# Early up-products for every pair, operands split ahead of two stage borders, and a modulation vector summed by columns, in a two-layer hybrid decoder

## The chip, the cores and the metric

The kernel runs on one core of one Trainium2 chip. The metric is the device time in microseconds of one execution, taken as the median of several. The engines are called as the profile calls them: PE is TensorE (PEld its weight loads), DVE is VectorE, ACT is ScalarE, POOL is GpSimd, and SP is the queue that issues nearly all DMAs.

## What is computed

Two layers of a decoder over 1024 tokens of width 1024, all in float32. Each layer has a token-mixing part and a channel-mixing part, each between two norms, with a scale, a shift and a gate that come from a vector `c`:

```python
mod = silu(c) @ ada_w[l] + ada_b[l]          # six vectors of 1024: shift, scale, gate, twice
h = rms_norm(x, g_pre_mix) * (1 + scale_m) + shift_m
q, k, v, u = split(h @ w_in + b_in)          # 512, 128, 128, 512 columns
mix = concat([window_attention(rotary(q), rotary(k), v), pool_mixer(u)]) @ w_out
x = x + gate_m * rms_norm(mix, g_post_mix)
h = rms_norm(x, g_pre_ffn) * (1 + scale_f) + shift_f
f = (silu(h @ w_gate) * (h @ w_up)) @ w_down # inner width 2816
x = x + gate_f * rms_norm(f, g_post_ffn)
```

## The kernel before

**Number format.** Every operand of a large product is split into two float32r parts: `split` (L211) lets ACT round it to `hi` (L213), and DVE subtracts to get `lo` (L214). `mm3` (L238) then issues three matmuls, hi·hi (L239), hi·lo (L242) and lo·hi (L243). A product can thus start when ACT has made `hi`, and goes on when DVE has made `lo`.

**Channel mixing.** The tokens are two halves of 512. The two large products of channel mixing are each done in a seven-product scheme (Strassen-Winograd), with the token half and the halves of the inner dimension as the two-by-two blocks. There are `NPAIR` = 11 pairs of 128-column blocks of the inner dimension. For each pair the up stage needs seven products; `double` (L989) is one of them, 24 matmuls. Two of the seven, with the right operands `B11` and `B21`, use only the first token half. For the first `sum(FIRST)` pairs they are made early by `up_firsts` (L1009): it loads the pair's first 128 columns of `w_gate` and `w_up`, adds the two products (L1034, L1036), sends the sum to DRAM (`firsts_x`, L1038), applies the gate function (L1006, L1007) and sends that as `a11` (L1042). `up_pair` (L1045) later loads these two back (L1057, L1058). A pair that was not done early makes both products itself (L1073 to L1082), so that it has seven products and not five.

**Order of the stages in one layer.** (1) q, k and v of half 0; (2) u of half 0 and attention and pooling of half 0, beside the projections of half 1; (3) the output projection of half 0 and its norm; (4) `u_pass` of half 1 beside `first_half` (L1368), which transposes the normed half 0 into eight pieces `hT`; (5) `firsts[0]`, early products for three pairs, beside attention and pooling of half 1; (6) the output projection of half 1; (7) `firsts[1]`, early products for six more pairs, beside `second_norm` (L1398), which norms half 1 and builds the 40 right operands `T2`, `T1`, `T3`, `B22`, `T4` of the up stage in `up_sums` (L971, on DVE, ACT and POOL); (8) the up stage, `up_pair` for 11 pairs; (9) the down stage, `down` (L1134), seven products over 11 pairs, in which the other half's last norm and the next layer's first pieces are made (`between`, L1458). At the end of layer 0 `post_ffn` (L538) finishes half 1.

**What sets the order.** `run` (L596) steps one main stream and lets side streams step at given rates; this is the written order. A scheduler then orders each engine's instructions, so that what is ready early can move ahead of what was written before it; each engine works its own list strictly in that order. Memory is taken from pools by tag with a fixed number of buffers; `region` (L109) frees one stage's pool and opens the next one's in the same bytes, and a tile there waits until the tiles it covers are done. `raw`, `hi`, `lo`, `ph`, `ar`, `sa`, `sb`, `fn`, `hT` and `ada` are shared by all stages; `bh` and `bl` belong to the region `down`, `cfa` and `cfb` to `mix`, the right operands `t1` to `t4` to `up`.

**The places that the change touches.** `up_firsts` splits its first operand (L1023) before its first product; the stream's first step is taken after `first_half` is done. `down` splits the first left operand (`left_of`, L1182) and right operand (L1220, into `bh` and `ph`) after the region `up` is closed. `ada_pair` (L359) makes the scale and the shift: `ada_sum` (L260) multiplies 128 × 512 blocks of `ada_w` with `c` on DVE, adding eight of them into `acc` (L271, L273), splits `acc` into two `ph` tiles, and two matmuls with a one-column selector (`picks`, L367, L368) sum over partitions; after four such rows one copy and four transposes (L375) bring the result into columns. For layer 1's first norm this runs beside the down stage of layer 0, at three steps for each of the 20 its four rows have, over 77 steps of the main stream: `(side, 3 * len(jobs) * ADA)` is 60. `normalise` (L456) scales a half by its inverse norm; at the end of layer 0 the half 1 goes from there to DRAM (L465) and comes back transposable, 128 columns at a time (L481), in the next layer's `u_pass`.

Of the kernel before, what the change touches and what calls it, by code (L numbers as in the profile page):

```python
# [20 lines left out]
P = 128  # L21
# [44 lines left out]
def hybrid_decoder_kernel(  # L66
# [193 lines left out]
    def ada_sum(l, n0, got):  # L260
# [22 lines left out]
        got += [t_("ph", [P, 512], F32R), t_("ph", [P, 512], F32R)]  # L283
        split(*got, acc)
# [104 lines left out]

    gates = {}  # L390
# [31 lines left out]
    def ada_stream(jobs):  # L422

        for l, n0, close in jobs:
            got = []
            yield from ada_sum(l, n0, got)
            close(*got)


    spill, normed = {}, {}  # L430
# [25 lines left out]
    def normalise(h, xs, rstd, keep=False):  # L456

        dst = None if keep else dr.tile([T, D], F32, tag=f"n{h}", name=f"n{h}", bufs=2)
        for t in range(NT):
            if t % 2 == 0:  # L460
                last = nc.vector.tensor_scalar(xs[t], xs[t], rstd[:, t : t + 1], None, op0=ALU.mult)
            else:
                nc.scalar.activation(xs[t], xs[t], AF.Copy, scale=rstd[:, t : t + 1])
            if not keep:
                nc.sync.dma_start(dst[t * P : (t + 1) * P, :], xs[t])  # L465
        normed[h] = dst
        return last

    def pre_norm_raw(h, k, ab, prev=None, xs=None, hf=None, bank=None):

        if bank is None:
            bank = transposed(h, k, prev, xs)
        hf = part("raw") if hf is None else hf
        scale, shift = ab[:, 0, k : k + 1], ab[:, 1, k : k + 1]
        nc.scalar.activation(hf, bank, AF.Identity, bias=shift, scale=scale)
        return hf

    def transposed(h, k, prev=None, xs=None):
        if xs is None:
            xk = part("raw").rearrange("p (t n) -> p t n", t=NT)  # L480
            nc.sync.dma_start(  # L481
                xk, normed[h].rearrange("(t p) n -> p t n", p=P)[:, :, k * P : (k + 1) * P]
            )
            src = [xk[:, t, :] for t in range(NT)]
        else:
            src = [xt[:, k * P : (k + 1) * P] for xt in xs]
# [7 lines left out]
    def pre_norm_piece(h, k, ab, prev=None, xs=None, keep=None, hf=None, bank=None):  # L494

        hf = pre_norm_raw(h, k, ab, prev, xs, hf, bank)
# [6 lines left out]

    def load_residual(h, tag="cfa"):

        xs = []
        for t in range(NT):
            if t % 2 == 0:
                big = t_(tag, [P, 4, T]).rearrange("p (t i) n -> p t (i n)", t=2)
            nc.sync.dma_start(big[:, t % 2, :], spill[h][t * P : (t + 1) * P, :])  # L510
            xs.append(big[:, t % 2, :])
        return xs

    def post_norm(h, fn, ss, xs):
# [15 lines left out]
        normalise(h, fn, inv_rms(sq), True)  # L530
# [7 lines left out]
    def post_ffn(h, fn, ss, G, keep):  # L538
# [15 lines left out]
        normalise(h, fn, inv_rms(sq), keep)  # L554
# [579 lines left out]
    def down(l, wd, load, kept, fn, ended, last):  # L1134
# [47 lines left out]
        def left_of(a, p0, p1, c0, c1):  # L1182

            n, w = p1 - p0, c1 - c0
            raw, lh, ll = (
                part(tag, 2 * w).rearrange("p (i n) -> p i n", n=w)[:, :n, :] for tag in ("raw", "hi", "lo")
            )
            nc.sync.dma_start(raw, kept[a][:, p0:p1, c0:c1])
            split(lh, ll, raw)
            return lh, ll  # L1190

# [18 lines left out]
        for name, a, right, evict in jobs[:-1]:  # L1210
            banks = [acc_bank() for _ in range(NT)]
            for g, (p0, p1) in enumerate(DOWN_GROUPS):
                n = p1 - p0
                lh, ll = left_of(a, p0, p1, 0, T)
                src = right(g)
                rights = []
                for i in range(n):
# [15 lines left out]
        for ts in ((0, 1), (2, 3)) if last else (range(NT),):  # L1233
            banks = {t: acc_bank() for t in ts}
            for g, (p0, p1) in enumerate(DOWN_GROUPS):
                n = p1 - p0
                lh, ll = left_of(a, p0, p1, ts[0] * P, (ts[-1] + 1) * P)
# [37 lines left out]
    normalise(0, xs, stats(xs, t_("rs", [P, 8])), True)  # L1275
# [5 lines left out]
    def first_pieces(b):  # L1281
        ks = (2 * b, 2 * b + 1)
        bank = transposed(0, ks[0], None, xs)
        ada_first_ab(b * CW, acc, par["cols"], par["abm"])
        for k, bank in zip(ks, (bank, None)):
            hf = t_("uT", [P, HALO + T])[:, :T]
            hts[0].append(pre_norm_piece(0, k, par["abm"], None, xs, None, hf, bank))
# [25 lines left out]
    normalise(1, xs1, rstd1, True)  # L1313
# [5 lines left out]
    FIRST = (3, 6)  # L1319
    for l in range(DEPTH):  # L1320
        cols = par["cols"]
        if l:
            region("mix")
# [3 lines left out]
        def piece_read(k, ins):  # L1327
            pieces[k] = pre_norm_piece(1, k, par["abm"], ins, None if l else xs1)
# [46 lines left out]
        pre = first_half()  # L1375
# [3 lines left out]
        ops = {B11: hts0[:HK], B21: hts0[HK:]}  # L1379
# [18 lines left out]
        def second_norm():  # L1398
# [3 lines left out]
            for k in range(HK):  # L1402
                f0, f1 = (
                    pre_norm_raw(1, kk, par["abf"], None, fn, part_)
# [29 lines left out]

        region("down")
# [22 lines left out]
        def between():  # L1458
# [10 lines left out]
            yield from post_ffn(0, fn[0], ss[0], G, True)  # L1469
# [47 lines left out]
```

## Time and profile before

| | |
|---|---|
| median of 3 runs | 1948.76 us (1945.44 to 1952.4) |
| the profiled execution, its own time | 1944.55 us |
| its span, first to last instruction | 1942.8 us |
| mean granted TensorE clock | 0.993 |
| busy: PE, DVE, ACT, POOL | 1874.0, 1564.3, 954.5, 49.0 us |
| DMA | 336.62 MB, mean 173 GB/s |

In the views, a row of a timeline gives the start and the length in us, the engine, the line, the operation, what it writes and reads, and in brackets how long its engine stood idle before it and who ended that. A row of the windows gives, for a stretch, each engine's busy time with the number of its instructions (the x in brackets), the clock that TensorE was granted (PEclk, 1.00 is full), and the share and rate of the DMA engines. Matmul records overlap, because they are pipelined: the time from the start of one to the start of the next is the pitch, and it is shorter than a record.

The stages of layer 0 end at about 75 (q, k, v), 275 (stage 4), 433 (stage 7), 762 (up) and 990 us (down); those of layer 1 at about 1232 (stage 4), 1388 (stage 7), 1720 (up) and 1943 us.

### The profile page before, as it was taken

Reading aid. Unit: us, or ns where it says so; the run is one execution under the profiler, and the core shown is the slowest. Engines: PE = TensorE matmul, PEld = TensorE weight load, DVE = VectorE, ACT = ScalarE, POOL = GpSimd, SP = SyncE. Lnnn points to the kernel's source line nnn. Section 1 sums busy time; section 2 is a strip of 40 time slices with the busy share of each in tenths; the row PEclk is TensorE's granted clock in tenths of the full one; section 3 lists DMA queues with packets and bytes.
Section 4 is the critical chain, followed back from the end, with each engine's and each line's share of the span. In section 5 each row is a group of like instructions: output and inputs, shape, how many; then the busy total and the mean of one; then the engine's idle time right before and its main releaser. Section 6 shows DMA issues by size and latency. Waiting matters only on the chain. (4 is left out here: it accounts for less than half of the span.)

```text
span 1942.8 us, 26040 instructions
## 1 busy us (share of the span) xinstructions
PE 1874.0 (96%) x8958; PEld 1541.0 (79%) x8958; DVE 1564.3 (81%) x2907; ACT 954.5 (49%) x1794; POOL 49.0 (3%) x100
## 2 busy tenths in 40 slices
PE   6999999999999999999999999999999999999997
PEld 4887778878888887778887878888778888878886
DVE  5999986779889886887878998756988888667687
ACT  4776785652222223445657668755522222235452
POOL 1000000020000000000000000000200000000000
PEclk9999999999999999999999999999999999999999
DMA  9345463556455446842556455535554644474343
GB/s 324 98 156 161 163 204 125 182 184 203 163 173 176 167 163 240 301 131 83 189 171 203 132 176 180 172 120 195 187 177 158 220 165 152 163 263 149 114 140 110
DMA packets 222052, 336.62 MB, mean 173 GB/s; under 512 B 16696, under 2 KB 120008, under 8 KB 221920
## 3 DMA queue, kind: packets, MB, share of 16 engines
q1 hardware_dynamic: 221776, 334.92, 52.2%
q8 instruction: 70, 1.15, 0.2%
q14 instruction: 62, 0.51, 0.1%
q0 software_dynamic: 32, 0.00, 0.0%
q10 hardware_dynamic: 112, 0.04, 0.0%
HBM read 262.00 MB, written 72.89 MB: 172 GB/s over the span
## 5 line engine op out<-in xcount | busy, mean ns | idle before, releaser
L213 ACT ACTIVATE hi<-raw 128x1024 fp32r<-128x1024 f32 (+1 forms) x388 | 332.5, 869 | 377.8 <-PE acc L242 220.7
L214 DVE TENSOR_TENSOR lo<-raw,hi 128x1024 fp32r<-128x1024 f32 (+1 forms) x388 | 382.9, 993 | 113.4 <-ACT hi L213 112.6
L239 PE MATMUL acc<-t,hi 128*128 128x512 f32 x704 | 276.7, 393 | 5.7 <-ACT hi L213 5.7
L243 PE MATMUL acc<-t,lo 128*128 128x512 f32 x704 | 276.1, 393 | 3.4 <-DVE lo L214 3.4
L242 PE MATMUL acc<-t,hi 128*128 128x512 f32 x704 | 276.0, 392 | 0.0
L243 PE MATMUL acc<-bh,lo 128*128 128x512 f32 x528 | 206.4, 391 | 0.0
L239 PE MATMUL acc<-bh,hi 128*128 128x512 f32 x528 | 203.5, 390 | 3.0 <-ACT bh L213 3.0
L239 PE MATMUL acc<-hT,hi 128*128 128x512 f32 x480 | 191.2, 398 | 7.8 <-ACT hi L213 7.2
L1068 DVE TENSOR_TENSOR fn<-acc,fn 128x512 f32<-128x512 f32 x220 | 151.1, 687 | 50.8 <-PE acc L243 50.2
L242 PE MATMUL acc<-hT,hi 128*128 128x512 f32 x480 | 188.3, 392 | 0.0
L243 PE MATMUL acc<-hT,lo 128*128 128x512 f32 x480 | 186.8, 393 | 0.9 <-DVE lo L214 0.9
L239 PEld LDWEIGHTS acc<-t,hi 128*128 128x128 f32 x704 | 133.5, 190 | 34.9 <-ACT hi L213 7.3
L243 PEld LDWEIGHTS acc<-t,lo 128*128 128x128 f32 x704 | 133.4, 190 | 34.2 <-DVE lo L214 6.5
L242 PEld LDWEIGHTS acc<-t,hi 128*128 128x128 f32 x704 | 133.5, 190 | 27.9
L242 PE MATMUL acc<-ph,hi 128*128 128x512 f32 x320 | 126.0, 394 | 1.3 <-DVE ph L214 1.1
L239 PEld LDWEIGHTS acc<-bh,hi 128*128 128x128 f32 x528 | 99.1, 188 | 24.6 <-ACT bh L213 3.8
L273 DVE SCALAR_TENSOR_TENSOR ada<-ar,c_act,ada 128x512 f32<-128x512 f32 x140 | 104.7, 748 | 17.0 <-DMA ar<-in_ada_w_dram 15.8
L243 PEld LDWEIGHTS acc<-bh,lo 128*128 128x128 f32 x528 | 99.6, 189 | 20.5
L239 PEld LDWEIGHTS acc<-hT,hi 128*128 128x128 f32 x480 | 90.7, 189 | 27.4 <-ACT hi L213 9.1
L1006 ACT ACTIVATE fn<-fn 128x512 f32<-128x512 f32 x44 | 27.9, 633 | 168.9 <-DVE fn L1068 168.9
L243 PEld LDWEIGHTS acc<-hT,lo 128*128 128x128 f32 x480 | 90.1, 188 | 19.5 <-DVE lo L214 1.3
L242 PEld LDWEIGHTS acc<-hT,hi 128*128 128x128 f32 x480 | 90.7, 189 | 17.3 <-issue 0.2
(302 smaller groups left out, 3866.6 us busy)
## 6 DMA issues: line engine op xcount, KB each, us to landing
ar<-in_ada_w_dram SPq DMA_DIRECT2D x160, 256.0 KB
raw<-in_w_gate_dram SPq DMA_DIRECT2D x44, 512.0 KB
raw<-in_w_up_dram SPq DMA_DIRECT2D x44, 512.0 KB
raw<-in_w_in_dram SPq DMA_DIRECT2D x80, 256.0 KB
raw<-keeps SPq DMA_DIRECT2D x40, 512.0 KB
keeps<-fn SPq DMA_DIRECT2D x66, 256.0 KB
two_b<-in_w_down_dram SPq DMA_DIRECT2D x30, 512.0 KB
raw<-keepa SPq DMA_DIRECT2D x25, 512.0 KB
```

What stands on the lines that cost most here:

```text
L213: nc.scalar.activation(hi, src, AF.Copy)
L214: nc.vector.tensor_sub(lo, src, hi.bitcast(F32))
L239: ins = nc.tensor.matmul(dst, lh, rh, start=first, stop=False)
L242: nc.tensor.matmul(dst, lh, rl, start=False, stop=False)
L243: return nc.tensor.matmul(dst, ll, rh, start=False, stop=last)
L273: nc.vector.scalar_tensor_tensor(acc, w, c_act[:, i : i + 1], acc, op0=ALU.mult, op1=ALU.add)
L1006: nc.scalar.activation(g, g, AF.Silu)
L1068: nc.vector.tensor_add(halves_of(dst)[m], bank, halves_of(src)[m])
```

## The change

Five edits, whose line numbers are those of the changed file where they are not in the kernel above.

1. `FIRST` goes from (3, 6) to (3, 8): early products for all 11 pairs. `second_norm`'s 12 steps are spread over 16 products instead of 12.
2. The first operand of `firsts[0]` is loaded and split inside `first_half`, after the sixth of the eight pieces, and not after all of them.
3. `down_prelude` loads and splits the down stage's first left and right operand before the region `up` is closed; the right one goes to two `ph` tiles instead of `bh` and `ph`. With edit 1 the right operands `hT` are also free when the early products end.
4. For layer 1's first norm `ada_columns` takes the place of `ada_pair`: `acc` isn't split; its four 128 × 128 blocks are the stationary operands of matmuls with a column of ones, whose sums land as columns. Its side stream has 28 steps over the 77 instead of 60.
5. At the end of layer 0 the region `mix` is opened before half 1's last norm, and `normalise` writes into two `cfb` tiles there; the next layer's transposes read them (as layer 0 reads its input), with no way through DRAM.

```diff
-    FIRST = (3, 6)
+    FIRST = (3, NPAIR - 3)
...
             for k in range(KD):
-                hts0.append(pre_norm_piece(0, k, par["abf"], None, fn, kept0[k]))
+                hts0.append(pre_norm_piece(k, par["abf"], None, fn, kept0[k]))
+                if k == KD - 3:
+                    next(firsts[0])
                 yield
...
-        run(firsts[0], 1 + 2 * FIRST[0], (att, ATT_STEPS), (pool, POOL_STEPS))
+        run(firsts[0], 2 * FIRST[0], (att, ATT_STEPS), (pool, POOL_STEPS))
...
+    def down_prelude(wd, kept):
+        left = left_of(kept["a11"], *DOWN_GROUPS[0], 0, T)
+        right = t_("ph", [P, 512], F32R), t_("ph", [P, 512], F32R)
+        split(*right, wd[B11][0][:, 0, :])
+        return left, right
...
+        prelude = down_prelude(wd, kept)
         region("down")
...
+    def ada_columns(l, sub, cols, ab):
+        def close(r, acc):
+            bank = msc_bank()
+            for i in range(4):
+                nc.tensor.matmul(
+                    bank[:, i : i + 1], acc[:, i * P : (i + 1) * P], ones[:, 0:1], start=True, stop=True
+                )
+            m, o = r // 2, slice(r % 2 * 4, r % 2 * 4 + 4)
+            k0 = (3 * sub + 1 - m) * KD
+            nc.vector.tensor_add(ab[:, m, o], bank[:, 0:4], cols[:, k0 + o.start : k0 + o.stop])
+            if m == 0:
+                ada_scale(ab, sub, o, cols)
...
-            jobs = ada_pair(l + 1, 0, nxt["cols"], nxt["abm"])
+            jobs = ada_columns(l + 1, 0, nxt["cols"], nxt["abm"])
...
-            (between(), 7 * NPAIR), (side, 3 * len(jobs) * ADA),
+            (between(), 7 * NPAIR), (side, 28),
         )
         if nxt:
-            drain(post_ffn(1, fn[1], ss[1], G, False))
+            region("mix")
+            xs1 = wide_tiles("cfb")
+            drain(post_ffn(1, fn[1], ss[1], G, xs1))
```

What it moves shows in the engines' lists. The first place is DVE in layer 0 where `firsts[1]` ends and the up stage begins. `t_...`, `b` and the sums into `ar` and `sa` at L979 and L984 are `up_sums`; L1036 adds the last early product; L1083, L1084 and the `lo<-raw` behind them prepare the first product of the up stage. Before:

```order
L214 TENSOR_TENSOR t_4507<-sa,t_4506 128x512
L214 TENSOR_TENSOR t_4539<-ar,t_4538 128x512
L1007 TENSOR_TENSOR sb<-sb 128x512
L1083 TENSOR_TENSOR raw<-raw 128x8x128
L979 TENSOR_TENSOR ar<-sa,ar 128x512
L214 TENSOR_TENSOR b_4533<-sa,b_4532 128x512
L1084 TENSOR_TENSOR raw<-raw 128x8x128
L214 TENSOR_TENSOR t_4517<-ar,t_4516 128x512
L214 TENSOR_TENSOR t_4525<-sa,t_4524 128x512
L984 TENSOR_TENSOR sa<-sa,ar 128x512
L214 TENSOR_TENSOR lo<-raw,hi 128x1024
L214 TENSOR_TENSOR t_4509<-sa,t_4508 128x512
```

In the changed kernel the same place of DVE's list (L1054 is the addition of the early product, L1101, L1102 and L1106 are the preparations):

```order
L214 TENSOR_TENSOR t_4584<-sa,t_4583 128x512
L214 TENSOR_TENSOR t_4616<-ar,t_4615 128x512
L1054 TENSOR_TENSOR sb<-acc,sa 128x512
L1025 TENSOR_TENSOR sb<-sb 128x512
L1101 TENSOR_TENSOR raw<-raw 128x8x128
L271 TENSOR_SCALAR ada<-ar,c_act 128x512
L1102 TENSOR_TENSOR raw<-raw 128x8x128
L273 SCALAR_TENSOR_TENSOR ada<-ar,c_act,ada 128x512
L1106 TENSOR_TENSOR raw<-raw 128x8x128
L214 TENSOR_TENSOR lo<-raw,hi 128x1024
L273 SCALAR_TENSOR_TENSOR ada<-ar,c_act,ada 128x512
L1054 TENSOR_TENSOR sb<-acc,sa 128x512
```

All of `up_sums` now stands ahead of the preparations, and the first product's `lo` ahead of the last early product's additions; operations of the next modulation vector (`ada`) have moved in between.

The second place is ACT in layer 0 behind `u_pass` of half 1 (`uT` are its results). `raw<-msc` and `hT<-raw` are pieces of `first_half`, and `hi<-raw 128x1024` is the operand of the first early product. Before:

```order
L684 ACTIVATE uT<-acc,cols 128x512 x4
L475 ACTIVATE raw<-msc,colp 128x512 x2
L213 ACTIVATE hT<-raw 128x512 x2
L475 ACTIVATE raw<-msc,colp 128x512
L213 ACTIVATE hi<-raw 128x1024
L213 ACTIVATE hT<-raw 128x512
```

In the changed kernel:

```order
L702 ACTIVATE uT<-acc,cols 128x512 x4
L495 ACTIVATE raw<-msc,colp 128x512 x2
L213 ACTIVATE hT<-raw 128x512
L213 ACTIVATE hi<-raw 128x1024
L213 ACTIVATE hT<-raw 128x512
L495 ACTIVATE raw<-msc,colp 128x512
```

The operand has moved ahead by one `hT` split and one `raw` copy. PE's list is the same in both kernels up to the first early product.

The third place is SP's list at the start of layer 0's up stage in the changed kernel; L1071 loads the weights of a pair, `ar<-in_ada_w_dram` those of the modulation, and `hT<-in_w_down_dram` the right operand `B11` of the down stage:

```order
L1076 DMA sa<-keepa_2926 128x512
L280 DMA ar<-in_ada_w_dram 128x512
L1147 DMA hT<-in_w_down_dram 128x512
L1147 DMA hT<-in_w_down_dram 128x2x512
L1056 DMA firsts<-sa 128x1024
L280 DMA ar<-in_ada_w_dram 128x512 x2
L1147 DMA hT<-in_w_down_dram 128x2x512
L1076 DMA sa<-keepa_2926 128x512
L1060 DMA keepa_2926<-sb 128x512
L1147 DMA hT<-in_w_down_dram 128x2x512
L1071 DMA raw<-in_w_gate_dram 128x4x256
L1071 DMA raw<-in_w_up_dram 128x4x256
```

The loads of `B11` stood at the end of the up stage before; now four of the six stand ahead of the second pair's weights.

More of the change, by code (lines that the diff above doesn't have):

```diff
@@ L282, in ada_sum @@
                 yield
-        got += [t_("ph", [P, 512], F32R), t_("ph", [P, 512], F32R)]
-        split(*got, acc)
+        if whole:
+            got.append(acc)
+        else:
+            got += [t_("ph", [P, 512], F32R), t_("ph", [P, 512], F32R)]
+            split(*got, acc)
         yield
@@ L388, in ada_pair @@
         ]
+    def ada_columns(l, sub, cols, ab):
[10 more added lines that the diff above has]
+                ada_scale(ab, sub, o, cols)
+        return [
+            (l, (3 * sub + 1 - r // 2) * D + r % 2 * 512, lambda acc, r=r: close(r, acc), True)
+            for r in range(4)
+        ]
     gates = {}
@@ L422, in ada_stream @@
     def ada_stream(jobs):
[L424 removed]
+        for l, n0, close, *whole in jobs:
             got = []
[L426 removed]
+            yield from ada_sum(l, n0, got, *whole)
             close(*got)
[L430 removed]
+    spill = {}
     for h in range(NHALF):
@@ L476, in pre_norm_raw, with transposed @@
         return hf
[L478 to L486, printed above, removed]
+    def transposed(k, prev, xs):
+        src = [xt[:, k * P : (k + 1) * P] for xt in xs]
         bank = msc_bank()
@@ L536, in scaled_add, with post_ffn @@
         nc.vector.tensor_add(fn, fn, xt)
-    def post_ffn(h, fn, ss, G, keep):
+    def post_ffn(h, fn, ss, G, into=None):
         rstd = inv_rms(ss)
@@ L553, in post_ffn @@
         spill[h] = new
-        normalise(h, fn, inv_rms(sq), keep)
+        normalise(fn, inv_rms(sq), into)
         yield
@@ L1132, in down_loads, with left_of, down @@
         return wd, load
-    def down(l, wd, load, kept, fn, ended, last):
+    def left_of(a, p0, p1, c0, c1):
+        n, w = p1 - p0, c1 - c0
+        raw, lh, ll = (
+            part(tag, 2 * w).rearrange("p (i n) -> p i n", n=w)[:, :n, :] for tag in ("raw", "hi", "lo")
+        )
+        nc.sync.dma_start(raw, a[:, p0:p1, c0:c1])
+        split(lh, ll, raw)
+        return lh, ll
+    def down_prelude(wd, kept):
[3 more added lines that the diff above has]
+        return left, right
+    def down(l, wd, load, kept, fn, ended, last, prelude):
         (c11, c12), (c21, c22) = [[[c[:, i * 512 : (i + 1) * 512] for c in fn[h]] for i in range(2)] for h in range(2)]
@@ L1213, in down @@
                 n = p1 - p0
[L1214 to L1217, printed above, removed]
+                if name == "p1" and g == 0:
+                    (lh, ll), *rights = prelude
+                else:
+                    lh, ll = left_of(kept[a], p0, p1, 0, T)
+                    src = right(g)
+                    rights = []
+                for i in range(len(rights), n):
                     rights.append((t_("bh", [P, 512], F32R), t_("ph" if count[0] % 5 < 3 else "bl", [P, 512], F32R)))
@@ L1327, in piece_read @@
         def piece_read(k, ins):
-            pieces[k] = pre_norm_piece(1, k, par["abm"], ins, None if l else xs1)
+            pieces[k] = pre_norm_piece(k, par["abm"], ins, xs1)
         qkvs = {h: [] for h in range(NHALF)}
```

74 lines of the change are left out of this document (33 added, 41 removed).

## The prediction

> **What bounds the kernel now.** I read the page's busy times first, then a calm stretch of the windows as a yardstick, then PE's waits, and last the windows and timeline around each border.
>
> ```profile
> span 1942.8 us, 26040 instructions
> PE 1874.0 (96%) x8958; PEld 1541.0 (79%) x8958; DVE 1564.3 (81%) x2907; ACT 954.5 (49%) x1794; POOL 49.0 (3%) x100
> ```
>
> PE is the bound on average, and only 69 us of the span are without a matmul. None of the five edits removes a large product, so what can be won is where PE stands still or runs below its usual pace. The yardstick is layer 1's up stage:
>
> ```profile
> 1432.00:1720.00 288.00, 288.00 (x1271) 237.65 (x1269) 233.50 (x299) 77.71 (x90) 0.00 (x0) 1.00 0.50 169
> ```
>
> Here PE is full at a full clock: 288.00 / 1271 = 0.2266 us for each matmul. For any other stretch of 128 × 512 matmuls, the lost time is its width less 0.2266 times its matmuls; this counts idle time and slow clock together. Now the waits of PE (columns: total us, times, longest):
>
> ```profile
> PE acc L239 <- ACT hi L213: 14.6, 9, 3.1
> PE msc L367 <- ACT ph L213: 3.7, 6, 1.4
> PE acc L239 <- ACT bh L213: 3.0, 2, 1.5
> PE msc L368 <- DVE ph L214: 2.3, 3, 1.3
> PE msc L489 <- DMA raw<-n: 1.3, 1, 1.3
> ```
>
> Each of these has an edit: `hi` late (edits 1 and 2), `bh` late (3), `ph` of the modulation late (4), half 1's way through DRAM (5). They add up to 24.9 us, and the stretches around them lose more than the waits themselves. They are on the path, because PE's list is in order and nothing else is due there.
>
> **Edit 1, early products to up stage.**
>
> ```profile
> 430.00:447.00 17.00, 13.75 (x46) 10.00 (x45) 16.82 (x22) 7.79 (x11) 3.75 (x2) 0.80 0.47 157
> 1386.00:1403.00 17.00, 13.00 (x43) 9.36 (x42) 16.85 (x20) 8.24 (x12) 3.73 (x2) 0.80 0.42 140
> ```
> ```profile
> 434.71 0.50 PE L239 MATMUL acc<-t,hi 128*128 128x512 f32 x1 [1.75 <-ACT hi L213]
> 436.57 0.79 PE L243 MATMUL acc<-t,lo 128*128 128x512 f32 x1 [1.12 <-DVE lo L214]
> ```
> ```profile
> 431.25 2.32 DVE L1084 TENSOR_TENSOR raw<-raw 128x1024 f32<-128x1024 f32 x1
> 435.30 1.21 DVE L214 TENSOR_TENSOR lo<-raw,hi 128x1024 fp32r<-128x1024 f32 x1
> 438.34 0.69 DVE L214 TENSOR_TENSOR t<-ar,t 128x512 fp32r<-128x512 f32 x1
> ```
>
> DVE is full (16.82 of 17.00) while PE waits: the releaser `hi` of ACT is itself fed by DVE's L1084, which ended at 433.57. DVE is still in `up_sums` until 438.34 + 0.69 = 439.03, while PE's first idle began at 434.71 - 1.75 = 432.96. DVE is 6.1 us behind. The stretch loses 17.00 - 46 × 0.2266 = 6.6 us in layer 0 and 17.00 - 43 × 0.2266 = 7.3 us in layer 1.
>
> Two pairs more are four products of 24 matmuls, 96 × 0.2266 = 21.8 us more under which DVE can finish. DVE gets work with them: I allow per product one `lo` (1.21) and two additions (0.69), 10.4 us for four, and four modulation steps that moved in, at 0.748:
>
> ```profile
> L273 DVE SCALAR_TENSOR_TENSOR ada<-ar,c_act,ada 128x512 f32<-128x512 f32 x140 | 104.7, 748 | 17.0 <-DMA ar<-in_ada_w_dram 15.8
> ```
>
> 21.8 - 10.4 - 3.0 = 8.4 us, more than the 6.1 it is behind, with 2.3 to spare. What is late next is the operand after the border, whose weights come by DMA. In layer 1 pair 1 already loses:
>
> ```profile
> 1426.00:1432.00 6.00, 4.15 (x18) 2.81 (x17) 6.00 (x9) 2.95 (x3) 0.00 (x0) 1.00 0.61 219
> 1416.65 1.23 DVE L1083 TENSOR_TENSOR raw<-raw 128x1024 f32<-128x1024 f32 x1 [2.66 <-DMA keepa<-sb]
> ```
>
> That is 6.00 - 18 × 0.2266 = 1.9 us, a leftover of the same backlog: DVE stood 2.66 us for a load, then was full. In sum 6.6 + 7.3 + 1.9 = 15.8 us; I keep 1.0 per layer for the first product's own wait, so **13.8** (6 if DVE catches up only by half, 15.8 at most).
>
> **Edit 3, up to down.**
>
> ```profile
> 760.00:766.00 6.00, 4.51 (x20) 3.42 (x19) 5.49 (x9) 4.30 (x7) 0.00 (x0) 1.00 0.95 299
> 763.62 1.20 PE L239 MATMUL acc<-bh,hi 128*128 128x512 f32 x4 [1.49 <-ACT bh L213]
> 1718.00:1724.00 6.00, 4.51 (x20) 3.38 (x20) 5.49 (x10) 4.30 (x7) 0.00 (x0) 1.00 0.91 295
> ```
>
> Each stretch loses 6.00 - 20 × 0.2266 = 1.5 us, all of it the wait for `bh`, whose memory lay under the last up operand. Split into `ph` it is ready before. I keep 0.2 each for the buffer it now shares: **2.6** (0 to 3.0).
>
> **Edit 4, the modulation by columns.**
>
> ```profile
> 796.00:847.00 51.00, 45.85 (x190) 35.66 (x189) 43.76 (x60) 21.89 (x37) 0.00 (x0) 0.97 0.74 246
> 839.21 0.39 PE L367 MATMUL msc<-ph,picks 128*4 128x512 f32 x1 [1.35 <-ACT ph L213]
> 840.89 0.39 PE L368 MATMUL msc<-ph,picks 128*4 128x512 f32 x1 [1.29 <-DVE ph L214]
> 43.61 0.61 PE L344 MATMUL msc<-ones_r,ar 128*128 128x1 f32 x5
> ```
>
> The four rows of the modulation put ACT's and DVE's splits into PE's path; the stretch loses 51.00 - 190 × 0.2266 = 7.9 us, about 1.7 of it the pace of the small matmuls themselves (eight at 0.2266). The new sums need no split. Their price has a near row: one-column f32 matmuls with a 128 × 128 weight, five in 0.61 us, 0.12 each. Sixteen products in two records each are 32 × 0.12 = 3.8 us; eight removed `picks` matmuls (1.8) and the transposes (some 0.5) go off, net 1.5. I keep 1.0 for waits on `acc`. 7.9 - 1.5 - 1.0 = **5.4** (2 to 7).
>
> **Edit 2, `u_pass` to early products.**
>
> ```profile
> 272.00:279.00 7.00, 5.00 (x19) 3.93 (x19) 4.98 (x12) 7.00 (x18) 0.00 (x0) 0.76 0.67 221
> 275.37 0.80 PE L239 MATMUL acc<-hT,hi 128*128 128x512 f32 x1 [2.00 <-ACT hi L213]
> 1229.00:1236.00 7.00, 5.00 (x29) 3.93 (x28) 5.94 (x18) 7.00 (x19) 0.33 (x1) 1.00 0.69 228
> 1231.90 0.50 PE L239 MATMUL acc<-hT,hi 128*128 128x512 f32 x1 [2.00 <-ACT hi L213]
> ```
> ```profile
> 273.56 0.81 ACT L475 ACTIVATE raw<-msc,colp 128x512 f32<-128x512 f32 x1
> 274.22 1.09 ACT L213 ACTIVATE hi<-raw 128x1024 fp32r<-128x1024 f32 x1
> ```
>
> ACT is full (7.00 of 7.00), so its order decides. The operand moves ahead of one copy (273.56 to 274.22, a pitch of 0.66) and one `hT` split (some 0.54, as a 512-column split is half of the 1.09): 1.2 us earlier in each layer, 2.4. In layer 0 the idle is also followed by slow clock: 0.76 over 7.00 us is 0.24 × 7.00 = 1.7 us. With 0.8 us of idle left I take two thirds of that, 1.1. Together **3.5** (1 to 5.7, the whole idle and clock). The two `hT` pieces that it passes are needed only for the last of the product's eight groups of matmuls.
>
> Short idles cost clock only sometimes: after the same 2.00 us the clock was 0.76 in one layer and 1.00 in the other, and 0.80 at both borders above. [...]
>
> **Edit 5, layer 0 to layer 1.**
>
> ```profile
> 1024.00:1043.00 19.00, 15.59 (x88) 12.00 (x88) 16.09 (x60) 14.25 (x32) 0.00 (x0) 1.00 0.60 182
> ```
>
> PE is idle for 19.00 - 15.59 = 3.4 us around the read-back of half 1; 1.3 of that is the wait for `raw<-n` above, which goes. Of the other 2.1, short waits for `hi`, `lo` and a norm, I take half: **2.3** (0 to 3.4).
>
> **What it adds.**
>
> ```profile
> raw<-in_w_gate_dram SPq DMA_DIRECT2D x36, 256.0 KB
> firsts<-sa SPq DMA_DIRECT2D x18, 512.0 KB
> fn<-firsts SPq DMA_DIRECT2D x18, 512.0 KB
> hT<-in_w_down_dram SPq DMA_DIRECT2D x10, 512.0 KB
> ```
>
> These are for 18 early pairs: each has two weight loads of 0.25 MB for `w_gate` and as many for `w_up`, the sum's way out and back at 0.5 MB, and 0.25 MB for `a11`'s return, 2.25 MB. Four pairs more are 9 MB; edit 5 saves 4 MB. 5 MB at the 0.50 share of the yardstick stay under PE's work: **0**. `B11`'s loads move to the start of the up stage, five of 512 KB in each layer and one of 256, 2.8 MB, and SP's queue is in order, so the second pair's weights stand behind them.
>
> ```profile
> 450.00:460.00 10.00, 10.00 (x46) 8.27 (x45) 8.31 (x12) 1.70 (x2) 0.00 (x0) 1.00 1.01 354
> ```
>
> There the DMA is already full, at 354 GB/s, with PE full. The moved loads cost 2.8 MB / 354 GB/s = 7.9 us per layer of that rate. Each pair's five products last 5 × 24 × 0.2266 = 27 us and its loads are issued that much ahead, so I price it at 0, at most 7.9 per layer.
>
> **Sum.** 13.8 + 2.6 + 5.4 + 3.5 + 2.3 = 27.6 us. The profiled execution took 1944.55 us (1.75 beyond its span) and becomes 1917; it lay 4.2 under the median of the runs shown, on whose basis the forecast is 1948.8 - 27.6 = **1921 us**. Differences under 0.3%, 5.8 us, can't be told from no change.
>
> **The rivals.** *A: the border isn't cured.* DVE's spare is only 2.3 us by my count, and all of `up_sums` now stands ahead of the first product's preparations in its list; if it is still late there, PE waits as before and only 0 to 6 of the 13.8 come. For it: DVE is full in the row above. Against it: 21.8 us of new cover. The gain is then 10 to 20, 1929 to 1939; chance 0.22. In this case I count another (0.07 of the 0.22): that the slow clock is not made by these stalls at all. Its part in the sum is 0.20 × 17.00 twice and 1.7, 8.5 us; without it the gain is 19 and the time 1930. [...]
>
> *B: slower, by the loads at the start of the up stage.* `B11`'s 2.8 MB and the modulation's loads stand in SP's queue ahead of the second pair's weights, at a place with DMA at 1.01. If those weights land late, PE waits for each pair until the queue is drained. It decides when landing is put off by more than the gain, over (27.6 + 5.8) / 2 = 17 us a layer; twice the 7.9, so each load would also have to wait for a buffer. The time is then over 1955; chance 0.05. For it is the 2.66 us wait of DVE on a DMA; against it the 0.50 share after 1432.
>
> *C: nothing.* The re-made lists bring new waits of `ph`, `raw` or `msc` buffers in down and at the borders, each of about the 1.3 us of the `ph` waits, and a dozen of them and a few us of B take the gain back: 1943 to 1954, 0.08.
>
> **How the numbers follow.** Forecast, gain 20 to 35 (1914 to 1929): 0.58. A: 0.22. A gain of 6 to 10: 0.04. C: 0.08. B: 0.05. Over 35, when the whole of the bounds comes: 0.03. Faster 0.58 + 0.22 + 0.04 + 0.03 = 0.87, same 0.08, slower 0.05. The range takes in the forecast and A, and at its low end the sum of the upper bounds, 15.8 + 3.0 + 7 + 5.7 + 3.4 = 34.9, which is 1914, with 2 us for the median: 1912 to 1939.
>
> **What would show it.** Right: after the early products PE's `acc<-t,hi` waits under 0.5 us at a clock of 1.00; no `bh` wait; no `picks` rows beside layer 0's down; `raw<-n` gone; the first early product's idle 0.8. Wrong: DVE still in `up_sums` when the up stage begins; DVE's L1101 waiting for a DMA longer than 2.66 us at the second pair; new waits for `ph` or `acc` in the down stage.

## The result, and the profile after

The changed kernel takes 1928.63 us (median of 4 runs, 1928.41 to 1929.62) against 1948.17 us for the kernel before: ratio 0.9905, 95% interval 0.9891 to 0.9918, a gain of 16 to 21 us. Run again beside the last experiments it took 1928.44 us (6 runs), ratio 0.9913, 0.9893 to 0.9933. The forecast was 1921 us in a range of 1912 to 1939: the sign and the range held, but about 8 us of the forecast 27.6 did not come. The profiled execution took 1928.41 us, 16.1 under that of before.

The page's first lines after:

```profile
span 1926.6 us, 26083 instructions
PE 1867.8 (97%) x8978; PEld 1540.6 (80%) x8978; DVE 1559.5 (81%) x2906; ACT 949.8 (49%) x1789; POOL 49.1 (3%) x100
```

PE's waits (total us, times, longest):

```profile
PE acc L239 <- ACT hi L213: 9.9, 10, 2.2
PE acc L243 <- DVE lo L214: 5.6, 7, 1.1
PE msc L370 <- ACT ph L213: 1.4, 3, 0.7
```

The waits for `bh` and for `raw<-n` are gone, and those for `picks` (now L370) are down to 1.4 us. The wait for `hi` fell only from 14.6 to 9.9, and that for `lo` at L243 rose from 4.3 to 5.6. The windows show where:

```profile
272.00:279.00 7.00, 5.87 (x31) 4.41 (x30) 5.30 (x12) 6.72 (x16) 0.00 (x0) 1.00 0.69 205
279.00:286.00 7.00, 5.81 (x30) 4.29 (x29) 3.69 (x11) 5.00 (x11) 0.24 (x1) 1.00 0.91 275
451.00:469.00 18.00, 16.12 (x64) 12.62 (x63) 16.79 (x21) 5.24 (x6) 0.00 (x0) 0.91 0.94 306
1396.00:1413.00 17.00, 14.34 (x61) 10.85 (x60) 15.36 (x20) 5.24 (x6) 0.00 (x0) 1.00 0.90 297
780.00:850.00 70.00, 70.00 (x318) 58.19 (x317) 58.61 (x77) 32.81 (x52) 0.00 (x0) 1.00 0.64 213
```

In the part of layer 0's down stage where the modulation runs, the last row, PE has no gap left. The two starts of the up stage, the third and fourth row, still have 1.9 and 2.7 us of PE idle, and the clock is still 0.91 in layer 0. In the first early products, the first two rows, the idle of 2.00 us at 273 us has shrunk, but there is a new gap in the second row, where before PE was busy for all of the 7.00 us.

For the experiments I cut every trace at the same instructions on PE: the start of `u_pass` of half 1, of `firsts[1]`, of the first product of the down stage, and of the next layer. This leaves out the first stretch, up to `u_pass`, which no edit touches and which lay between 232.2 and 237.2 us in the fourteen traces; whole-kernel times carry that scatter. One profiled execution each, in us (the up stage is taken together with `firsts[1]`, so that it holds the same products whatever `FIRST` is):

| kernel | median | `u_pass` to `firsts[1]`, layer 0, 1 | `firsts[1]` to down, layer 0, 1 | down, layer 0 | next layer to its 2nd `u_pass` |
|---|---|---|---|---|---|
| before | 1948.2 | 129.40, 128.00 | 399.95, 402.92 | 225.30 | 201.91 |
| changed | 1928.6 | 129.25, 129.32 | 396.96, 396.15 | 217.55 | 200.78 |
| changed, once more | 1928.4 | 128.88, 129.24 | 398.11, 396.83 | 217.47 | 198.42 |
| edit 1 undone | 1936.2 | 129.36, 128.81 | 399.22, 401.60 | 217.50 | 198.69 |
| edit 2 undone | 1930.1 | 129.50, 128.08 | 399.86, 397.94 | 217.50 | 200.24 |
| edit 3 undone | 1930.9 | 129.29, 131.15 | 399.43, 398.08 | 216.59 | 199.21 |
| edit 4 undone | 1931.7 | 129.26, 129.13 | 398.91, 398.85 | 223.68 | 200.12 |
| edit 5 undone | 1931.9 | 129.38, 131.36 | 397.13, 396.69 | 217.44 | 203.55 |
| columns, 60 steps | 1930.3 | 129.20, 129.01 | 396.01, 397.42 | 219.83 | 199.31 |
| splits, 28 steps | 1933.6 | 128.77, 129.28 | 396.15, 399.13 | 224.02 | 198.36 |
| edit 1 alone | 1944.6 | 129.44, 128.06 | 399.46, 399.26 | 226.59 | 201.49 |

The column of the down stage repeats to 0.1 us between kernels that share its code; the others scatter by 1 to 3 us. Ratios have intervals of about 0.0015 either way, 3 us, so a median alone doesn't settle an edit of 2 us.

### The profile page after: what moved, and what is told of

It is laid out like the page before. It is cut to its first block, busy times and chain, and to the rows that moved or that the text cites. A ratio compares the mean times of both kernels' runs of the same rounds, so it can differ in the third digit from the quotient of the medians.

```text
span 1926.6 us, 26083 instructions
## 1 busy us (share of the span) xinstructions
PE 1867.8 (97%) x8978; PEld 1540.6 (80%) x8978; DVE 1559.5 (81%) x2906; ACT 949.8 (49%) x1789; POOL 49.1 (3%) x100
## 4 chain that ended last, share of the span: by engine, by line
PE 74%; DVE 12%; DMA 6%; ACT 4%; issue 2%; POOL 0%; SPq 0%; DVEq 0%; ACTq 0%; POOLq 0%
PE acc L243 23%; PE acc L239 22%; PE acc L242 22%; DMA ar<-in_ada_w_dram 3%; DVE lo L214 2%; DVE ada L273 1%; DMA raw<-in_w_up_dram 1%; PE msc L832 1%; ACT hi L213 1%; PE msc L502 1%; PE pv L239 1%; PE pv L242 1%; DMA ar<-x 1%; DVE fn L541 1%; PE pv L243 1%
## 5 line engine op out<-in xcount | busy, mean ns | idle before, releaser
L243 PE MATMUL acc<-t,lo 128*128 128x512 f32 x704 | 275.4, 391 | 5.0 <-DVE lo L214 5.0
L243 PE MATMUL acc<-bh,lo 128*128 128x512 f32 x520 | 202.4, 389 | 0.0
L243 PE MATMUL acc<-hT,lo 128*128 128x512 f32 x480 | 186.2, 393 | 0.8 <-DVE lo L214 0.7
L243 PEld LDWEIGHTS acc<-t,lo 128*128 128x128 f32 x704 | 132.5, 188 | 35.0 <-DVE lo L214 7.6
L243 PEld LDWEIGHTS acc<-bh,lo 128*128 128x128 f32 x520 | 97.6, 188 | 20.4
L243 PEld LDWEIGHTS acc<-hT,lo 128*128 128x128 f32 x480 | 89.8, 188 | 20.4 <-DVE lo L214 2.5
```

What stands on the lines that cost most here:

```text
L243: return nc.tensor.matmul(dst, ll, rh, start=False, stop=last)
```

## The experiments

**The changed kernel once more**, with no edit, beside the last three kernels.

> The changed kernel once more, to stand beside the others on the same chip; 1928.6 us as measured, or 1930 to 1931 if the medians of 1930 to 1932 of the kernels with one small edit undone are this kernel's own scatter from one execution to the next.

1928.44 us (6 runs, 1927.08 to 1932.36). The first alternative holds for the median, which came again at 1928.4. But the ratios to the kernel before, run beside each, don't tell this kernel (0.9905 and 0.9913) from those with edit 2 undone (0.9909) or edit 3 undone (0.9907), or with the columns at the old pace (0.9899); what those edits are worth is read from the traces alone.

**Edit 1 undone.**

```diff
-    FIRST = (3, NPAIR - 3)
+    FIRST = (3, 6)
```

> The changed kernel with edit 1 alone undone: early products for 9 pairs again. Theory from the two traces: PE's loss where the up stage begins fell from 6.9 to 5.6 us in layer 0 and from 10.1 to 5.1 us in layer 1, so edit 1 was worth 6.3 us; undone, the time is 6.3 us over the changed kernel's 1928.6, 1934.9, with DVE full and PE waiting for hi where the up stage begins. Rival, the sum on record: edit 1 was worth 13.8 us and some 9 us were lost elsewhere; the time is then 1942.4.

1936.18 us (6 runs), ratio 0.9945, 0.9931 to 0.9959: 7.7 us over the changed kernel, near the theory's 6.3 and far from the rival's 13.8. In the table, the seven kernels that have both edit 1 and edit 3 take 397.6 us from `firsts[1]` to down in the mean, in both layers. With edit 1 undone this stretch is 1.6 us longer in layer 0, which lies within the scatter of the seven (396.0 to 399.9), and 4.0 us longer in layer 1, together 5.6. The old wait is back, in DVE's and ACT's work for the first product:

```profile
433.70 0.57 PE L239 MATMUL acc<-t,hi 128*128 128x512 f32 x1 [2.25 <-ACT hi L213]
435.56 0.79 PE L243 MATMUL acc<-t,lo 128*128 128x512 f32 x1 [0.85 <-DVE lo L214]
```

**Edit 1 alone**, put into the kernel before.

```diff
-    FIRST = (3, 6)
+    FIRST = (3, 8)
```

> The kernel before with edit 1 alone: early products for 11 pairs. Theory: DVE is no longer behind at the start of the up stage, but the first product's weights land late and lo stands behind other work on DVE, so 5 to 6 us are won, 1942 to 1943. Rival, the sum on record: 13.8 us, 1934.4.

1944.63 us (12 runs), ratio 0.9985, 0.9970 to 1.0001: 3 us, between nothing and 6; the table gives 0.5 + 3.7 = 4.2. Both ways of taking edit 1 put it at 3 to 8 us with the middle near 5, and 13.8 is out. The theory's size holds within the noise. Its cause shows in layer 0 of this trace: L1083 waits 1.4 us for its weights, and PE waits 0.49 us for `hi` and 0.84 for `lo` at the first product, 1.03 and 1.52 at the second pair.

**Edit 2 undone.**

```diff
-                if k == KD - 3:
-                    next(firsts[0])
...
-        run(firsts[0], 2 * FIRST[0], (att, ATT_STEPS), (pool, POOL_STEPS))
+        run(firsts[0], 1 + 2 * FIRST[0], (att, ATT_STEPS), (pool, POOL_STEPS))
```

> The changed kernel with edit 2 alone undone: the first early product's operand is split after all eight pieces. Theory from the two traces: the idle moved from the first to the second early product and the edit lost 1.2 us over both layers (0.15 won in layer 0, 1.3 lost in layer 1); undone, the time is 1927.4, and the 1.1 and 1.4 us waits for hi at the second early product are gone. Rival, the sum on record: the edit was worth 3.5 us; undone the time is 1932.1.

1930.12 us (5 runs), ratio 0.9909, 0.9895 to 0.9924, which can't be told from the changed kernel. In its own stretch the edit does lose: the three kernels without it have 129.4 and 128.0 us, the eleven others (three of them below) 129.2 and 129.6 in the mean, 0.3 won in layer 0 and 1.5 lost in layer 1. (Two of the eleven, with 131.15 and 131.36, lie 1.8 us and more above every other of them in the table; without them the loss in layer 1 is 1.2.) The changed kernel's timeline shows how, PE first, then ACT:

```profile
275.01 0.50 PE L239 MATMUL acc<-hT,hi 128*128 128x512 f32 x1 [0.81 <-ACT hi L213]
283.19 0.50 PE L239 MATMUL acc<-hT,hi 128*128 128x512 f32 x1 [1.13 <-ACT hi L213]
```
```profile
273.90 1.06 ACT L213 ACTIVATE hi<-raw 128x1024 fp32r<-128x1024 f32 x1
282.08 1.06 ACT L213 ACTIVATE hi<-raw 128x1024 fp32r<-128x1024 f32 x1 [1.88 <-DMA raw<-in_w_up_dram]
```

The first product starts 1.2 us earlier relative to the stream, as forecast. But the second operand's weights do not come earlier, ACT stood 1.88 us for their DMA, and PE waits 1.13 us (1.37 in layer 1): attention matmuls that stood between the matmuls of the first product before now stand behind the start of the second. With the edit undone both second waits are gone, and the first is 2.00 us again. That the total is not better without the edit goes, in its trace, with another place. At the start of the up stage DVE stood 4.54 us for a modulation load, behind which the second pair's preparation is queued, and PE waited at 484:

```profile
472.33 0.75 DVE L273 SCALAR_TENSOR_TENSOR ada<-ar,c_act,ada 128x512 f32<-128x512 f32 x1 [4.54 <-DMA ar<-in_ada_w_dram]
```
```profile
484.44 0.50 PE L239 MATMUL acc<-t,hi 128*128 128x512 f32 x1 [1.53 <-ACT hi L213]
486.70 0.80 PE L243 MATMUL acc<-t,lo 128*128 128x512 f32 x1 [1.52 <-DVE lo L214]
```

**Edit 3 undone.**

```diff
-        prelude = down_prelude(wd, kept)
         region("down")
...
-            down(l, wd, load, kept, fn, ended, not nxt, prelude), 7 * NPAIR,
+            down(l, wd, load, kept, fn, ended, not nxt, None), 7 * NPAIR,
```

> The changed kernel with edit 3 alone undone: the down stage's first operands are split after the up region is closed, the right one into bh. Theory and the sum on record agree within 0.4 us: the 1.49 us wait for bh returns in both layers, 3.0 us, 1931.6. Rival: the early loads of the right operands already bring that split forward, and nothing is lost, 1928.6.

1930.94 us (4 runs), ratio 0.9907, 0.9893 to 0.9920: 2.4 us by the medians, with 3 us of uncertainty. In layer 1 exactly the old wait returns. In layer 0 PE is held up as long, but 0.95 us of that time takes eight records of the modulation's column sums, which moved there out of the down stage, and 0.70 us is idle. By these waits the edit is worth 2.2 us, a little less than the theory's 3.0:

```profile
1708.51 1.20 PE L239 MATMUL acc<-bh,hi 128*128 128x512 f32 x4 [1.49 <-ACT bh L213]
```

**Edit 4 undone.**

```diff
-            jobs = ada_columns(l + 1, 0, nxt["cols"], nxt["abm"])
+            jobs = ada_pair(l + 1, 0, nxt["cols"], nxt["abm"])
...
-            (between(), 7 * NPAIR), (side, 28),
+            (between(), 7 * NPAIR), (side, 3 * len(jobs) * ADA),
```

> The changed kernel with edit 4 alone undone: the modulation by splits and picks, at 60 steps beside the down stage of layer 0. Theory from the two traces: the down stage of layer 0 became 7.8 us shorter, all of it by this edit; undone the time is 1936.4, with the ph waits back. Rival, the sum on record: 5.4 us, 1934.0, and the other 2.4 us came from the down stage's earlier loads.

1931.67 us (6 runs), ratio 0.9923, 0.9909 to 0.9938. The down stage of layer 0 is 223.68 - 217.5 = 6.2 us longer, in a column that repeats to 0.1; the medians differ by 3.2, with 3 us of uncertainty. I take 6.2, from one trace. The theory put all of the 7.8 us by which this stage became shorter down to this edit; the other 1.6 belong to other edits, and to which is open. The waits for `ph` are not where they were: PE now waits in the down stage's own products, for DVE's half of splits into the shared `ph`:

```profile
800.68 0.50 PE L242 MATMUL acc<-ph,hi 128*128 128x512 f32 x1 [1.44 <-DVE ph L214]
818.85 0.50 PE L242 MATMUL acc<-ph,hi 128*128 128x512 f32 x1 [1.51 <-DVE ph L214]
```

**The two halves of edit 4**, the columns at the old pace, and the splits at the new.

```diff
-            (between(), 7 * NPAIR), (side, 28),
+            (between(), 7 * NPAIR), (side, 3 * len(jobs) * ADA),
```

> The changed kernel with the columns, but 60 side steps as before. Theory: the splits and picks in PE's path were the cost, so the pace counts little, 1929 to 1930. Rival: the slower pace was what helped, as the modulation's loads and additions crowd DVE in the first part of the down stage; then some 6 us come back, 1935.

```diff
-            jobs = ada_columns(l + 1, 0, nxt["cols"], nxt["abm"])
+            jobs = ada_pair(l + 1, 0, nxt["cols"], nxt["abm"])
```

> The changed kernel with splits and picks again, but at 28 side steps. Theory: the four waits for ph remain, each 0.7 to 1.35 us twice, with the slow clock behind them, 1935 to 1936.4. Rival: at the slower pace DVE and ACT have room and the waits go, 1930.

Columns at 60 steps: 1930.25 us (4 runs), ratio 0.9899, 0.9883 to 0.9915, and 219.83 in the down column, 2.3 over the changed kernel. Splits at 28 steps: 1933.57 us (5 runs), ratio 0.9923, 0.9910 to 0.9936, and 224.02, as bad as at 60. So the columns bring 223.68 - 219.83 = 3.9 us, and the slower pace 2.3 more, but only with the columns; each figure is from one trace. With the splits at the slower pace the waits for `ph` shrink, from 4.5 us in all to 1.5, as the rival said, but the time goes elsewhere: PE waits 2.26 us for half 0's last norm on ACT (L486), which stands in ACT's list behind a `hi` that waits for its load, and half clock follows that stall (0.51 from 960.7 to 964.2, which loses 1.7 us). Why that load is late in this kernel is not shown.

```profile
960.04 0.92 PE L502 MATMUL msc<-ident,fn 128*128 128x128 f32 x6 [2.26 <-ACT fn L486]
```
```profile
957.89 1.06 ACT L213 ACTIVATE hi<-raw 128x1024 fp32r<-128x1024 f32 x1 [3.79 <-DMA raw<-keepa]
958.85 1.13 ACT L486 ACTIVATE fn<-fn,rs 128x1024 f32<-128x1024 f32 x1
```

**Edit 5 undone**: half 1 goes through DRAM again.

```diff
-            region("mix")
-            xs1 = wide_tiles("cfb")
+            xs1 = dr.tile([T, D], F32, tag="n1", name="n1", bufs=2)
             drain(post_ffn(1, fn[1], ss[1], G, xs1))
+            region("mix")
```

(`normalise` stores each tile to `xs1`, and `transposed` loads 128 columns back into `raw`, as before.)

> The changed kernel with edit 5 alone undone: half 1 goes through DRAM between the layers. Theory from the two traces: the layer border up to the second u pass became 1.1 us shorter; undone the time is 1929.7, with one wait of some 1.3 us for the read-back. Rival, the sum on record: 2.3 us, 1930.9. Further rival: 4 MB less traffic beside the down stage's end counts too, 1932 or more.

1931.91 us (5 runs), ratio 0.9929, 0.9917 to 0.9941: 3.4 us. The last column of the table agrees: 203.55, 201.91 and 201.49 in the three kernels that go through DRAM, 199.2 in the mean of the eleven that don't, 3.1 us. The wait itself is 1.5:

```profile
PE msc L509 <- DMA raw<-n: 1.5, 1, 1.5
```

My theory had read 1.1 us off one pair of traces, and the changed kernel's was the longest of its kind; the third expectation, that more than the wait is won, is the nearest in size. That the 4 MB less of traffic did it, as that expectation has it, no run separates from the short waits for `hi`, `lo` and the norm in the same stretch.

**What is left at the start of the up stage.** In the changed kernel PE waits there for `hi`, then `lo`, and for `lo` again in the second pair:

```profile
456.16 0.50 PE L239 MATMUL acc<-t,hi 128*128 128x512 f32 x1 [0.76 <-ACT hi L213]
458.01 0.50 PE L243 MATMUL acc<-t,lo 128*128 128x512 f32 x1 [1.11 <-DVE lo L214]
493.93 0.50 PE L243 MATMUL acc<-t,lo 128*128 128x512 f32 x1 [1.02 <-DVE lo L214]
```

and DVE's list there reads, with the last of `up_sums` in the first row:

```profile
449.60 0.69 DVE L214 TENSOR_TENSOR t<-ar,t 128x512 fp32r<-128x512 f32 x1 [0.15 <-ACT t L213]
...
452.26 1.23 DVE L1101 TENSOR_TENSOR raw<-raw 128x1024 f32<-128x1024 f32 x1 [0.57 <-DMA raw<-in_w_up_dram]
453.40 0.48 DVE L271 TENSOR_SCALAR ada<-ar,c_act 128x512 f32<-128x512 f32 x1
453.80 1.22 DVE L1102 TENSOR_TENSOR raw<-raw 128x1024 f32<-128x1024 f32 x1
454.94 0.75 DVE L273 SCALAR_TENSOR_TENSOR ada<-ar,c_act,ada 128x512 f32<-128x512 f32 x1
455.60 1.22 DVE L1106 TENSOR_TENSOR raw<-raw 128x1024 f32<-128x1024 f32 x1
456.73 1.22 DVE L214 TENSOR_TENSOR lo<-raw,hi 128x1024 fp32r<-128x1024 f32 x1
```

`up_sums` is done at 450.29, 5 us before PE runs out of early products at 455.40; the forecast's 2.3 us to spare was short. What is late is the pair's own preparation: DVE waits for the weights until 452.26, a modulation step stands between the two subtractions that `hi` needs, and another and L1106 stand ahead of `lo`. Three kernels took this apart.

The first orders `lo` ahead of L1106 in every pair, and the modulation's first step behind the first pair's third operand:

```diff
-        nc.vector.tensor_sub(a12, a12, a11)
+        after(nc.vector.tensor_sub(a12, a12, a11), made[-1])
...
-                    nc.vector.tensor_scalar(acc, w, c_act[:, 0:1], None, op0=ALU.mult)
+                    ins = nc.vector.tensor_scalar(acc, w, c_act[:, 0:1], None, op0=ALU.mult)
+                    if behind:
+                        after(ins, behind.pop())
```

(`made` holds the `lo` operations of the pair, `behind` the third one of the first pair.)

> The changed kernel with two edges added to DVE's order: in each pair of the up stage lo goes ahead of the subtraction at L1106, and the modulation's first multiplication goes behind the first pair's third operand. Theory: what is left of the loss where the up stage begins is DVE's order, not its load: hi comes 0.4 us earlier and lo 2.0 us earlier in each layer, of which PE can use about 1.2 with its idle of 0.8 and 1.1; with the 1.0 us of the second pair the gain is 2.3 to 4 us, 1924.6 to 1926.3. Rival: the weights' loads set the start, and nothing changes, 1928.6.

1931.44 us (4 runs), ratio 0.9913, 0.9899 to 0.9927: no gain. The waits for `lo` at the start fell to 0.53 us, but `firsts[1]` to down is 398.65 and 400.71, since later pairs' operands now hold PE in mid stage: in layer 0 it waits 1.25 and 0.94 us for `hi` and 1.03 for `lo`, where the changed kernel waits for none. The second kernel has the first of the two edges alone:

> The changed kernel with one edge added to DVE's order: in each pair of the up stage lo goes ahead of the subtraction at L1106; the modulation stays where it was. Theory: the first product's wait for lo falls from 1.1 to 0.5 us and the second pair's from 1.0 to 0.3, 2.4 to 2.6 us over both layers, and without the waits for hi in mid stage that the moved modulation brought: 1926 to 1928 where the changed kernel has 1928.6. Rival: the shorter waits are taken up by the next operand, no difference.

1940.73 us (12 runs), ratio 0.9968, 0.9953 to 0.9983: 12 us slower than the changed kernel. The first waits did shrink, but `firsts[1]` to down is 403.77 and 403.99. So it was not the moved modulation that brought the waits in mid stage: PE waits for `hi` four times, 4.8 us in all, between 510 and 740 us, where the changed kernel has no wait of this kind. PE, ACT and DVE of this kernel in mid stage (L1108 and L1109 are L1106 and L1107 of the changed kernel):

```profile
607.15 0.51 PE L239 MATMUL acc<-t,hi 128*128 128x512 f32 x1 [1.76 <-ACT hi L213]
```
```profile
606.04 2.96 ACT L213 ACTIVATE hi<-raw 128x1024 fp32r<-128x1024 f32 x3 [4.12 <-DVE raw L1109]
```
```profile
598.84 1.22 DVE L214 TENSOR_TENSOR lo<-raw,hi 128x1024 fp32r<-128x1024 f32 x1
...
602.98 1.21 DVE L1108 TENSOR_TENSOR raw<-raw 128x1024 f32<-128x1024 f32 x1
604.11 0.68 DVE L1025 TENSOR_TENSOR fn<-fn 128x512 f32<-128x512 f32 x1
604.71 1.22 DVE L1109 TENSOR_TENSOR raw<-raw 128x1024 f32<-128x1024 f32 x1
```

Behind `lo` the subtraction falls behind five more operations, and both subtractions then stand right before the next `hi`. The order that costs a microsecond at the start of the stage saves some 6 us in each layer over the later pairs. (No run has the edge in the first pair alone.)

The third kernel has this edge too, and puts the load of the early sum behind the pair's weights:

```diff
-            nc.sync.dma_start(X, xs[p])
+            after(nc.sync.dma_start(X, xs[p]), loaded)
```

> As the kernel before in this list, and in each pair of the up stage the load of the early sum (L1075, 0.5 MB) is put behind the pair's weights on SP's queue. Theory: the first product's start is set by its weights' landing, with DMA at 0.98 and 320 GB/s beforehand; 0.5 MB less in front is 1.6 us, so DVE's L1101 doesn't wait for DMA, the first wait for hi of 0.8 us goes, and the time falls by 1 to 2 us more. Rival: DVE's own work before L1101 sets it, and hi comes no earlier.

1939.02 us (12 runs), ratio 0.9966, 0.9953 to 0.9979: slower as a whole, by the same waits in mid stage, so the time forecast for it was wrong. But its start of the stage answers the question:

```profile
447.74 1.22 DVE L1105 TENSOR_TENSOR raw<-raw 128x1024 f32<-128x1024 f32 x1
448.87 0.68 DVE L1025 TENSOR_TENSOR sb<-sb 128x512 f32<-128x512 f32 x1
449.48 1.22 DVE L1106 TENSOR_TENSOR raw<-raw 128x1024 f32<-128x1024 f32 x1
```
```profile
453.10 0.50 PE L243 MATMUL acc<-t,lo 128*128 128x512 f32 x1 [0.23 <-DVE lo L214]
```

L1105 (L1101 of the changed kernel) has no DMA wait, the wait for the first `hi` is gone in both layers, where the kernel with the DVE edge alone still waits 0.64 and 1.16 us, and the one for `lo` is 0.23. It is not the modulation step between the two subtractions that made the difference: L1025 now stands in its place, and from the start of the first to the end of the second it takes 3.0 us here and 2.8 there. So the first product's start was set by the landing of its weights, and by L1025 (0.69 us), which stood ahead of L1101 before. `firsts[1]` to down is 403.39 and 405.75 us, though, and in layer 0 PE waits 1.37 us for `lo` at the very next product. A version with this edge on SP's queue, without the one on DVE, would be the one to try; no run here had it, and its gain, 1.6 us by the two waits for `hi` of the changed kernel (0.76 and 0.86), is an estimate.

## Why the prediction was right, and where it was off

The main reasoning held: PE is the bound, no large product goes, and what is won is the idle around the places edited. Three of the five terms came out near their size, and two were too high. That the time still fell into the range is in part its width, which took in rival A; and the terms as measured add up to some 16 us, at the low end of the interval of the total (16 to 21).

| edit | forecast | measured | from |
|---|---|---|---|
| 1, early products | 13.8 | 4 to 6 (3 to 8) | undone, alone, table |
| 2, first operand earlier | 3.5 | about -1 in its place | table; total not told apart |
| 3, down operands | 2.6 | 2.2 to 3.0 | waits back when undone; waits gone |
| 4, columns | 5.4 | 6.2 | down column |
| 5, half 1 on chip | 2.3 | 3.1 to 3.4 | undo, table |

**Edit 1, the step that failed.** "What is late next" was named, the operand after the border, but it was priced at 1.0 us a layer. It is 2.9 us of waits in layer 0 (0.76 + 1.11 + 1.02) and 3.7 in layer 1 (0.86 + 1.11 + 0.69 + 1.03), and 1.6 us of slow clock in layer 0: 8.2 us instead of 2.0. That is 6 of the 8 to 10 us that are missing; where the rest went is open. The argument about DVE's load was right and even too cautious: `up_sums` is out of the way 5 us before it is needed. But with it out of the way, the weights' landing and DVE's order set the start. The late weights are new: before, L1083 ran at 428.91 with no wait for a DMA.

**Rival A** has the size that was measured for edit 1, 0 to 6 us of 13.8, and the total of 1928.6 lies at the border between the forecast's case and it. Its mechanism did not happen: `up_sums` was not late. The case counted within it, that the slow clock is not made by these stalls, gave 1930, the nearest of all to the measured time, and by luck: most of the slow clock did go with the stalls, see below.

**Edit 2.** The step "1.2 us earlier in each layer" was right to 0.01 us (2.00 to 0.81 us of idle). What was missed is that the second operand had been covered by the same stretch of attention work, and that its weights land no earlier. The idle moved by one product. The 1.1 us for the slow clock did come: the window has 1.00 where it had 0.76.

**Edit 4.** The price of the columns was right: 8 matmul records in 0.95 us, 0.119 each, for the forecast 0.12.

```profile
799.50 0.95 PE L399 MATMUL msc<-ones_r,ada 128*128 128x1 f32 x8
```

The 1.0 us kept for waits on `acc` was not needed at 28 steps; at 60 it is (0.92 and 0.20 us were seen). That a third of the gain is the pace was not in the forecast. One reading was wrong: of the 7.9 us, 1.7 were put down to the pace of the small matmuls, but 190 × 0.2266 already counts these; of what is left beside the waits about half is slow clock, 0.97 over 51 us, 1.5 us. The sum does not change by it.

**Edits 3 and 5.** Edit 3 went as priced. Edit 5 brought 3.1 to 3.4, about all of the 3.4 us of idle that were read there; half of the small waits was too small a share, if the difference of 1 us is not noise.

**Rival B** did not happen: `B11`'s early loads were priced at nothing, and no wait of the second pair in the changed kernel is on its weights. But the zero for DMA as a whole was too low: with the DMA at 0.98 before the stage (one load of 512 KB less in front put L1101 1.5 us earlier, counted from the start of `firsts[1]`), it is a DMA that holds the first product, and a modulation load holds DVE for 3.7 us in the changed kernel:

```profile
472.07 0.75 DVE L273 SCALAR_TENSOR_TENSOR ada<-ar,c_act,ada 128x512 f32<-128x512 f32 x1 [3.67 <-DMA ar<-in_ada_w_dram]
```

**The slow clock.** The forecast let 6.8 us of slow clock at the two starts of the up stage go with the waits. In the trace after, 3.4 went in layer 1 (clock 1.00) and about half of 3.4 in layer 0 (0.91 of 18 is 1.6 us lost). Over the whole traces, their first 20 and last 10 us left out, the clock was half for 20.5 us before and for 6.8 after, so 6.8 of the 16.1 us between the two profiled executions are clock. The last section shows what went ahead of it in the two traces.

**The signs.** Of the signs of being right, four came: no `bh` wait, no `raw<-n`, no `picks` beside layer 0's down stage, and 0.81 us at the first early product. One did not: the waits for `hi` behind the early products are 0.76 and 0.86 us, not under 0.5, at a clock of 0.91 and 1.00. None of the signs of being wrong came.

## What to carry to other kernels

A loss at a stage border has several owners one behind the other. Before pricing the removal of the one that the profile names, go up the chain of the first product after the border to each of its inputs (the load, the preparing operations, the two parts of the split) and write down when each would be there if the named one took no time; the latest of these, and not zero, is what remains. Pulling an operand forward moved the wait to the next operand, whose load had not moved. And an order that looks wrong at a border may be what keeps the steady state free: here an edge meant for one place, put into every pair, cost 12 us.

## What the runs showed of the hardware

The granted clock after a short stall looks like chance: after the same 2.00 us it was 0.76 in layer 0 of the kernel before and 1.00 in layer 1. The traces of the two kernels show what went ahead of each drop to half. In both, the stretches of half clock begin whole multiples of 3.413 us apart (in the kernel before at 275.07, 435.50, 841.69 and 1391.23 us: 47, 119 and 161 of them; in the changed kernel at 151.44 and 458.64 us: 90), and each but the one at the end of the run lasts one or two of these, 3.41 or 6.83 us. So each trace can be cut into windows of that length. The first row below is the window that ends where the first half-clock stretch begins, and the second is that stretch; the last two are the two windows over which the same stall falls in layer 1:

```profile
271.66:275.07 3.41, 1.71 (x12) 1.20 (x11) 2.48 (x9) 3.41 (x6) 0.00 (x0) 1.00 0.79 229
275.07:278.49 3.42, 3.12 (x8) 2.55 (x9) 2.76 (x4) 3.42 (x13) 0.00 (x0) 0.50 0.57 219
1227.40:1230.81 3.41, 2.50 (x19) 1.98 (x17) 2.38 (x8) 3.41 (x7) 0.00 (x0) 1.00 0.79 207
1230.81:1234.22 3.41, 2.32 (x10) 1.75 (x11) 3.10 (x6) 3.41 (x11) 0.00 (x0) 1.00 0.70 269
```

In layer 0 all but a little of the stall lies in one window, in which PE stands still for 1.70 us, and half clock follows; in layer 1 it is divided, 0.91 and 1.09 us, and none follows. In the changed kernel the two waits at the start of the up stage, 0.76 + 1.11 us, add up in one window in layer 0, and 0.86 + 1.11 us fall into two in layer 1:

```profile
455.23:458.64 3.41, 1.53 (x7) 0.84 (x6) 3.41 (x5) 1.37 (x2) 0.00 (x0) 1.00 0.94 243
458.64:462.05 3.41, 3.41 (x10) 2.64 (x9) 3.41 (x6) 2.30 (x3) 0.00 (x0) 0.50 1.01 378
1397.31:1400.72 3.41, 2.64 (x12) 1.87 (x10) 3.41 (x5) 1.02 (x2) 0.00 (x0) 1.00 0.79 243
1400.72:1404.14 3.42, 2.22 (x8) 1.53 (x9) 3.42 (x5) 0.77 (x3) 0.00 (x0) 1.00 0.88 300
```

Counted over the windows at full clock of these two traces between 60 and 1900 us: half clock followed in all 3 in which PE was idle for more than 1.9 us, in 3 of the 5 with 1.5 to 1.9, and in none of the 1061 with less. So in these traces short stalls added up when they fell into one window, 1.70 us of idle in a window of 3.41 was enough once, and a stretch cost 1.7 us or 3.4 (half of 3.41 or 6.83). The windows do not lie at the same place in both traces: counted from the first instruction, those of the changed kernel are 0.75 us earlier. The same 2.00 us of stall fell into one window in one layer and into two in the other, so what a stall of 2 us will cost could not be told beforehand here; a stall well under 1.5 us, alone in its window, was not followed by half clock in either trace.
